# Products by channel with both parts of x in one matmul of 512 columns

## The chip, the cores and the metric

The kernel runs on one core of a Trainium2 chip. The metric is the device time of one execution in microseconds (us). The engines are named as in the profile: PE is TensorE's matmuls, PEld its weight loads, DVE is VectorE, ACT is ScalarE, POOL is GpSimd, SP the engine that issues the loads of weights.

## The reference

Two layers over 256 tokens of width 1024; each layer is a feed-forward block, a mixer and a second feed-forward block, and a norm ends it:

```python
for i in range(DEPTH):                      # DEPTH = 2
    h = h + 0.5 * swiglu_ffn(rmsnorm(h, norm_ffn1[i]), w_ffn1_in[i], w_ffn1_out[i])
    u = rmsnorm(h, norm_mix[i]) @ w_mix_in[i]          # 1024 -> 6232 columns
    z, xbc, dt_raw, q, k, v, q_idx, k_idx, w_idx = jnp.split(u, SPLIT_POINTS, axis=-1)
    y_ssd = ssd_mixer(z, xbc, dt_raw, conv_w[i], ...)  # convolution over time, masked sums, norm by group
    y_att = dsa_mixer(q, k, v, q_idx, k_idx, w_idx, positions)   # attention on the top 64 keys
    h = h + jnp.concatenate([y_ssd, y_att], axis=-1) @ w_mix_out[i]
    h = h + 0.5 * swiglu_ffn(rmsnorm(h, norm_ffn2[i]), w_ffn2_in[i], w_ffn2_out[i])
return rmsnorm(h, final_norm)
```

All is float32. The part that the change touches is the product of `rmsnorm(h)` with the columns of `z` (8 tiles of 128 channels) and of `xbc` (12 tiles) in the mixer's input projection.

## The kernel before

**Weights and products.** All weights, 214 MB, come from DRAM once, in blocks of 128 x 2048 numbers. A block lands in `raw`; ACT casts it to the matmul's reduced float32 (`whi`, L128) and DVE takes what is left over (`wlo` = raw - whi, L129). The operand x is held in the same way as a high and a low part (`tT` tiles, 32 of them of 128 x 256). Each product is made of three matmuls that add up in one PSUM bank: high with high, high with low, low with high (L186 to L188 in most places).

**By token and by channel.** Most products have the tokens on the partitions of the result: x is stationary, the weights stream past, 512 columns at a time. The columns of `z` and `xbc` are made by channel: 128 channels of the weights are stationary and the 256 tokens of x stream past (L915 to L917, 8 steps of 128 rows of the weights for each tile of channels). There are ten blocks of two such tiles in a layer, 20 tiles, 40 in the kernel. The list `MIX_ORDER` sets the order of these blocks and of the products for q, k, v and the small columns between them. In the profiled execution the first layer's stretch with products by channel lies between about 212 and 290 us.

**What becomes of a tile of channels.** `gate` (for `z`, L704) and `conv` (for `xbc`, L711) multiply the bank by `rb`, the row of the norm's factors, on DVE, into SBUF; this also empties the bank. `gate` then applies a silu on ACT. `conv` makes four steps (L718 on ACT, L720 on DVE three times) and a silu (L722 on ACT) into the tile `chan`. `by_token` transposes four such tiles on PE (L731) and scales them on DVE.

**The masked sums.** `ssd` makes, for each of two groups of eight heads, two sets of masks (four heads each): rows of cumulated sums are read back from DRAM into `s` by a DMA that POOL issues (L756), ACT makes differences and exponentials (L758 to L763), DVE multiplies (L764, L765), and PE makes the products of a set with the channels (L774, L778). `finish_y` goes on as deferred steps: `gated` scales y and multiplies by the gate, `sums` adds the squares on PE (L805) and takes the root on POOL (L809), `row` spreads the two numbers over a row by PE (L815, `rT`), and `scale` multiplies (L824 on DVE), casts (L826 on ACT) and takes the low part (L827 on DVE). The result is the first half of the operand of the out product. Attention's steps (L849 to L883) make the second half.

**What sets the order.** The code is written in program order with a planner, `flow`: after each unit of the main products it runs steps that were deferred by so many units, and one step of each generator (`ssd`, `attention`, the scores), a generator going on at its `yield`. A scheduler then puts every engine's instructions into one fixed queue; the hardware runs a queue strictly in its order. PSUM has four pools of two banks: `mm` and `ac` for main products, `sd` and `tp` for side steps.

Of the kernel before, what the change touches and what calls it, by code (L numbers as in the profile page):

```python
# [9 lines left out]
FR = mybir.dt.float32r  # L10
# [5 lines left out]
P = 128  # L16
D = 1024
L = 256
# [34 lines left out]
def hybrid_kernel(  # L53
# [12 lines left out]
    tT = ctx.enter_context(tc.tile_pool(name="tT", bufs=32))  # L66
# [26 lines left out]
    def ttile():  # L93
        return tT.tile([P, L], FR, name="tT", tag="tT")
# [88 lines left out]
    def three(ps, xhl, t, whi, wlo, first, last):  # L183

        xh, xl = (v[:, t * P:(t + 1) * P] for v in xhl)
        nc.tensor.matmul(ps, xh, whi, start=first, stop=False)  # L186
        nc.tensor.matmul(ps, xh, wlo, start=False, stop=False)  # L187
        nc.tensor.matmul(ps, xl, whi, start=False, stop=last)  # L188

# [159 lines left out]
    def setup():  # L349
# [4 lines left out]
        with tc.tile_pool(name="setup", bufs=1, reuse_waits="tile") as tmp:  # L354
# [22 lines left out]
            nc.tensor.transpose(pg[:, 0:64], rows, ident[:64, :64])  # L377
            nc.vector.tensor_copy(gains, pg[:, 0:64])
            nc.tensor.transpose(pg[:, 128:248], crows, ident[:120, :120])
# [49 lines left out]
    def split_scaled(ps, parts, t):  # L429

        parts = [([v[:, t * P:(t + 1) * P] for v in hl], g, ps[:, i * P:(i + 1) * P])
# [27 lines left out]
    class Norm:  # L459
# [14 lines left out]
        def turn(self, ps, t, c, pin=lambda ins: ins):  # L474
            if self.xT is None:
                self.xT = [(ttile(), ttile()) for _ in range(KD)]
# [94 lines left out]
    def mixer(l, norm, after):  # L571
        with ExitStack() as mctx:
# [130 lines left out]
            def gate(c, ps):  # L703
                nc.vector.tensor_mul(sz[:, c], ps, rb)  # L704
                nc.scalar.activation(sz[:, c], sz[:, c], AF.Silu)


            def conv(c, ps):
                xr = ms.tile([P, L + 3], F32, name="xr", bufs=2)
                nc.gpsimd.memset(xr[:, 0:3], 0.0)  # L710
                nc.vector.tensor_mul(xr[:, 3:], ps, rb)  # L711
# [26 lines left out]
            def ssd():  # L738
# [9 lines left out]
                for g in range(G_SSD):  # L748
                    ms4 = []
                    for h0 in (0, 4):  # L750
# [15 lines left out]
                        yield  # L766
                    half = xs[:, :, 512 * g:512 * g + 512]
# [15 lines left out]
            def finish_y(g, half, pss):  # L783
# [18 lines left out]
                def sums():  # L802
# [7 lines left out]
                    flow.defer(lambda: row(rg))  # L810
# [8 lines left out]
                def scale(rT):  # L819
                    for b in range(2):  # L820
                        for i in range(2):
                            k = 4 * g + 2 * b + i
                            hi, lo = ttile(), ttile()
# [4 lines left out]
                            yT[k] = (hi, lo)  # L828
# [4 lines left out]
            def attention():  # L833
                while bias[1] is None:
                    yield
                for hg in range(0, H_ATT, 4):
# [30 lines left out]
                    for h in range(5):  # L867
                        if h:
# [6 lines left out]
                            hi, lo = ttile(), ttile()  # L875
                            nc.scalar.copy(hi, po[:, 0:L])
                            nc.vector.tensor_sub(lo, po[:, 0:L], hi.bitcast(F32))
                            yT[8 + hg + h - 1] = (hi, lo)
# [28 lines left out]
            for what in MIX_ORDER:  # L907
                if isinstance(what, int):
                    hi, lo = stream.take()
                    for j in range(2):  # L910
                        ps = main_bank(True)[:, :L]
                        for k in range(KD):
                            o = k * 256 + j * P
                            xh, xl = norm.xT[k]
                            nc.tensor.matmul(ps, hi[:, o:o + P], xh, start=(k == 0), stop=False)  # L915
                            nc.tensor.matmul(ps, hi[:, o:o + P], xl, start=False, stop=False)  # L916
                            nc.tensor.matmul(ps, lo[:, o:o + P], xh, start=False, stop=(k == KD - 1))  # L917
# [119 lines left out]
```

## Time and profile before

| | |
|---|---|
| time of three runs, median (lowest to highest) | 1207.95 us (1207.37 to 1208.33) |
| the profiled execution: its time | 1208.47 us |
| the profiled execution: its span | 1206.8 us |
| PE busy | 1192.7 us, 99% of the span |
| PEld, DVE, ACT, POOL busy | 83%, 61%, 53%, 8% |
| TensorE's granted clock, mean | 0.999 of full speed (the 2.4 GHz level) |
| data read from HBM | 212.17 MB, 177 GB/s over the span |

The span is the time from the first to the last instruction of the profiled execution. Busy time of PE is modelled and counts a matmul until its end, while the next one starts earlier; so the cost of a matmul in a row of them is read from start to start, not from its duration. A wait is the time in which an engine had nothing to run, with the work that released it.

### The profile page before, as it was taken

What the parts mean: (1) busy time and instruction counts of PE and PEld (TensorE: products, weight loads), DVE (VectorE), ACT (ScalarE), POOL (GpSimd) and SP (SyncE); (2) the same over time, 40 slices, a digit from 0 to 9 for tenths busy, and PEclk for the clock granted to TensorE, in tenths of its full rate; (3) what the DMA queues carried; (4) which work ended last, traced back from release to release, by engine and by line L of the source; (5) the groups of instructions that cost most, each with busy time, mean ns of one, the idle gap of its engine ahead of it and who ended that gap; (6) DMA issues with size and microseconds to landing.
All of it is one profiled execution on the core that took longest, in us unless ns stands there. A gap on an engine that the chain in (4) does not pass through costs nothing.

```text
span 1206.8 us, 15519 instructions
## 1 busy us (share of the span) xinstructions
PE 1192.7 (99%) x6125; PEld 1002.6 (83%) x6125; DVE 738.4 (61%) x948; ACT 634.1 (53%) x847; POOL 101.9 (8%) x206
## 2 busy tenths in 40 slices
PE   9999999999999999999999999999999999999997
PEld 7788888998777888888888888899987788888886
DVE  5645545796797555544465554467868965554544
ACT  7544435658775544443354444366478555444432
POOL 1200000502410000000000000014133000000000
PEclk9999999999999999999999999999999999999999
DMA  9565555654534465555655645466455435556550
GB/s 291 171 205 184 186 175 165 210 175 158 192 140 145 135 210 187 164 207 188 196 161 188 201 163 198 163 205 196 145 191 192 140 122 174 191 164 204 183 200 36
DMA packets 152909, 214.26 MB, mean 178 GB/s; under 512 B 8068, under 2 KB 123012, under 8 KB 152836
## 3 DMA queue, kind: packets, MB, share of 16 engines
q1 hardware_dynamic: 151108, 207.99, 52.6%
q0 software_dynamic: 1280, 4.23, 1.0%
q8 instruction: 48, 0.79, 0.3%
q10 hardware_dynamic: 448, 1.05, 0.2%
q14 instruction: 25, 0.20, 0.1%
HBM read 212.17 MB, written 1.08 MB: 177 GB/s over the span
## 4 chain that ended last, share of the span: by engine, by line
PE 89%; ACT 5%; DMA 2%; DVE 1%; issue 1%; POOL 1%; SPq 0%; POOLq 0%; ACTq 0%
PE mm L187 14%; PE mm L188 13%; PE mm L186 13%; PE ac L188 11%; PE ac L187 11%; PE ac L186 11%; PE mm L915 2%; PE ac L915 2%; PE mm L917 2%; PE ac L916 2%; PE ac L917 2%; PE mm L916 2%; PE tp L541 2%; ACT whi L128 1%; PE sd L849 1%
## 5 line engine op out<-in xcount | busy, mean ns | idle before, releaser
L129 DVE TENSOR_TENSOR wlo<-raw,whi 128x2048 fp32r<-128x2048 f32 (+3 forms) x208 | 451.7, 2176 | 325.2 <-ACT whi L128 324.4
L128 ACT CAST whi<-raw 128x2048 fp32r<-128x2048 f32 (+3 forms) x208 | 376.8, 1818 | 285.5 <-PE ac L188 193.0
L186 PE MATMUL mm<-whi,tT 128*128 128x512 f32 (+1 forms) x640 | 255.2, 399 | 0.0
L187 PE MATMUL mm<-wlo,tT 128*128 128x512 f32 (+1 forms) x640 | 247.9, 387 | 0.9 <-DVE wlo L129 0.9
L188 PE MATMUL mm<-whi,tT 128*128 128x512 f32 (+1 forms) x640 | 248.1, 388 | 0.0
L186 PE MATMUL ac<-whi,tT 128*128 128x512 f32 (+1 forms) x448 | 176.5, 394 | 0.0
L188 PE MATMUL ac<-whi,tT 128*128 128x512 f32 (+1 forms) x448 | 173.3, 387 | 0.0
L187 PE MATMUL ac<-wlo,tT 128*128 128x512 f32 (+1 forms) x448 | 173.1, 386 | 0.0
L187 PEld LDWEIGHTS mm<-wlo,tT 128*128 128x128 f32 x640 | 120.6, 188 | 24.1 <-DVE wlo L129 1.4
L188 PEld LDWEIGHTS mm<-whi,tT 128*128 128x128 f32 x640 | 120.3, 188 | 24.4
L186 PEld LDWEIGHTS mm<-whi,tT 128*128 128x128 f32 x640 | 120.6, 188 | 23.5 <-issue 1.3
L188 PEld LDWEIGHTS ac<-whi,tT 128*128 128x128 f32 x448 | 84.3, 188 | 16.4
L187 PEld LDWEIGHTS ac<-wlo,tT 128*128 128x128 f32 x448 | 84.6, 189 | 15.4 <-DVE wlo L129 0.4
L186 PEld LDWEIGHTS ac<-whi,tT 128*128 128x128 f32 x448 | 84.3, 188 | 14.7
L186 PE MATMUL ac<-whi,hT_hi 128*128 128x512 f32 x176 | 69.3, 394 | 0.0
L186 PE MATMUL mm<-whi,hT_hi 128*128 128x512 f32 x176 | 69.0, 392 | 0.0
L188 PE MATMUL ac<-whi,hT_lo 128*128 128x512 f32 x176 | 68.6, 390 | 0.0
L188 PE MATMUL mm<-whi,hT_lo 128*128 128x512 f32 x176 | 68.6, 390 | 0.0
L187 PE MATMUL mm<-wlo,hT_hi 128*128 128x512 f32 x176 | 68.5, 389 | 0.0
L187 PE MATMUL ac<-wlo,hT_hi 128*128 128x512 f32 x176 | 68.5, 389 | 0.0
L450 POOL TENSOR_TENSOR r_x<-ms_x,mhalf 128x1 f32<-128x1 f32 x12 | 6.6, 547 | 670.7 <-DVE ms_x L448 663.2
L563 ACT ACTIVATE s1k<-mm,r_x 128x256 f32<-128x256 f32 x44 | 20.7, 471 | 69.7 <-PE mm L188 69.7
(230 smaller groups left out, 1604.6 us busy)
## 6 DMA issues: line engine op xcount, KB each, us to landing
raw<-in_w_ffn_in_dram SPq DMA_DIRECT2D x172, 512.0 KB, 4.9
raw<-in_w_ffn_out_dram SPq DMA_DIRECT2D x44, 1024.0 KB, 4.9
raw<-in_w_mix_in_dram SPq DMA_DIRECT2D x44, 1024.0 KB, 5.2
raw<-in_w_mix_out_dram SPq DMA_DIRECT2D x16, 1024.0 KB, 4.8
s<-csum POOLq DMA_DIRECT2D x8, 512.0 KB, 4.1
raw<-in_w_mix_in_dram SPq DMA_DIRECT2D x4, 600.0 KB, 3.9
raw<-in_w_mix_in_dram SPq DMA_DIRECT2D x4, 568.0 KB, 3.9
raw<-in_w_ffn_in_dram SPq DMA_DIRECT2D x8, 256.0 KB, 6.0
```

The lines of the kernel that those rows point to most:

```text
L128: pin(nc.scalar.copy(hi[:, o], raw[:, o]))
L129: pin(nc.vector.tensor_sub(lo[:, o], raw[:, o], hi[:, o].bitcast(F32)))
L186: nc.tensor.matmul(ps, xh, whi, start=first, stop=False)
L187: nc.tensor.matmul(ps, xh, wlo, start=False, stop=False)
L188: nc.tensor.matmul(ps, xl, whi, start=False, stop=last)
L450: nc.gpsimd.tensor_tensor(r, m, mhalf, ALU.pow)
L541: nc.tensor.transpose(ps[:, f * L + t * P:f * L + (t + 1) * P], hs[:, t, f * P:(f + 1) * P], ident)
L563: nc.scalar.activation(sg, ps[:, 0:256], AF.Silu, scale=norm.r[t])
L849: nc.tensor.matmul(ps[:, j * nk:(j + 1) * nk], qT[:, hg + h0 + j, t * P:(t + 1) * P], kT[:, hg + h0 + j, 0:nk], start=True, stop=True)
L915: nc.tensor.matmul(ps, hi[:, o:o + P], xh, start=(k == 0), stop=False)
L916: nc.tensor.matmul(ps, hi[:, o:o + P], xl, start=False, stop=False)
L917: nc.tensor.matmul(ps, lo[:, o:o + P], xh, start=False, stop=(k == KD - 1))
```

## The change

The tiles of x now hold both parts side by side, so that one matmul can stream 512 columns; the memory is the same.

```diff
-    tT = ctx.enter_context(tc.tile_pool(name="tT", bufs=32))
+    tT = ctx.enter_context(tc.tile_pool(name="tT", bufs=16))
...
-    def ttile():
-        return tT.tile([P, L], FR, name="tT", tag="tT")
+    def ttiles():
+
+        both = tT.tile([P, 2, L], FR, name="tT", tag="tT")
+        return both[:, 0], both[:, 1], both
...
+    def three_by_channel(ps, xhl, whi, wlo, first, last):
+
+
+        xh, both = xhl[0], xhl[2].rearrange("p a t -> p (a t)")
+        if not first:
+            nc.tensor.matmul(ps[:, :L], wlo, xh, start=False, stop=False)
+        nc.tensor.matmul(ps, whi, both, start=first, stop=last)
+        if first:
+            nc.tensor.matmul(ps[:, :L], wlo, xh, start=False, stop=False)
+
+    def join(dst, ps):
+        nc.scalar.copy(dst, ps[:, L:])
+        nc.vector.tensor_add(dst, ps[:, :L], dst)
...
                     for j in range(2):
-                        ps = main_bank(True)[:, :L]
+                        ps = main_bank(True)
                         for k in range(KD):
                             o = k * 256 + j * P
-                            xh, xl = norm.xT[k]
-                            nc.tensor.matmul(ps, hi[:, o:o + P], xh, start=(k == 0), stop=False)
-                            nc.tensor.matmul(ps, hi[:, o:o + P], xl, start=False, stop=False)
-                            nc.tensor.matmul(ps, lo[:, o:o + P], xh, start=False, stop=(k == KD - 1))
+                            three_by_channel(ps, norm.xT[k], hi[:, o:o + P], lo[:, o:o + P], k == 0, k == KD - 1)
```

So a step of a tile of channels has two matmuls instead of three: the high part of the weights with both parts of x, 512 columns into a whole bank, and the low part with the high part of x, 256 columns into the bank's first half. The halves are added on the way out: ACT copies the second half into the target, DVE adds the first half, and the multiplication by `rb` comes after that, from SBUF to SBUF.

```diff
             def gate(c, ps):
-                nc.vector.tensor_mul(sz[:, c], ps, rb)
+                join(sz[:, c], ps)
+                nc.vector.tensor_mul(sz[:, c], sz[:, c], rb)
                 nc.scalar.activation(sz[:, c], sz[:, c], AF.Silu)
...
-                nc.vector.tensor_mul(xr[:, 3:], ps, rb)
+                join(xr[:, 3:], ps)
+                nc.vector.tensor_mul(xr[:, 3:], xr[:, 3:], rb)
```

Three side steps change their place: the second transpose of the setup goes ahead of the first one's copy, a `yield` stands between the masks and the products of a group in `ssd`, and `row` is deferred by two units instead of one.

```diff
+            nc.tensor.transpose(pg[:, 128:248], crows, ident[:120, :120])
             nc.vector.tensor_copy(gains, pg[:, 0:64])
-            nc.tensor.transpose(pg[:, 128:248], crows, ident[:120, :120])
             nc.vector.tensor_copy(convs, pg[:, 128:248])
...
                         nc.vector.tensor_mul(m1, m1, bc(cb[:, g, L:384], [P, 4, P], 1))
                         yield
+                    yield
                     half = xs[:, :, 512 * g:512 * g + 512]
                     pss = [bank(ac) for _ in range(2)]
...
-                    flow.defer(lambda: row(rg))
+                    flow.defer(lambda: row(rg), 2)
```

How the queues change shows at three places of the first layer. On PE, at the first group's masked sums, where `s_` with a number is a set of masks, the kernel before has the second of the two sets (the first stands 24 matmuls of the main products earlier):

```order
L188 MATMUL mm<-whi,tT 128x512
L894 MATMUL tp<-ident,s_2901 128x128 x4
L774 MATMUL ac<-s_2887,s_1648 64x256 x2
L778 MATMUL ac<-s_2887,s_1648 64x128 x2
L774 MATMUL ac<-s_2887,s_1648 64x256 x2
L778 MATMUL ac<-s_2887,s_1648 64x128 x2
L186 MATMUL mm<-whi,tT 128x512
```

and the changed kernel (L793 and L797 are these lines there, L913 is L894, L188 to L190 are L186 to L188):

```order
L190 MATMUL mm<-whi,tT 128x512
L913 MATMUL tp<-ident,s_2765 128x128 x4
L793 MATMUL ac<-s_2677,s_1632 64x256 x2
L797 MATMUL ac<-s_2677,s_1632 64x128 x2
L793 MATMUL ac<-s_2677,s_1632 64x256 x2
L797 MATMUL ac<-s_2677,s_1632 64x128 x2
L793 MATMUL ac<-s_2751,s_1632 64x256 x2
L797 MATMUL ac<-s_2751,s_1632 64x128 x2
L793 MATMUL ac<-s_2751,s_1632 64x256 x2
L797 MATMUL ac<-s_2751,s_1632 64x128 x2
L188 MATMUL mm<-whi,tT 128x512
```

Both sets now stand together, where only the second one stood.

On ACT, after the evacuation of k's products (L944), the kernel before makes the masks of the second group (L758 to L763), squares y (L796), and evacuates a product that frees the bank for v (the L944 near the end):

```order
L758 ACTIVATE s_3047<-s_3047,cs 128x128 x2
L760 ACTIVATE s_3047<-s_3047,cs 128x256 x2
L758 ACTIVATE s_3047<-s_3047,cs 128x128 x2
L760 ACTIVATE s_3047<-s_3047,cs 128x256
L796 ACTIVATE s_1647<-s_1648 128x512
L760 ACTIVATE s_3047<-s_3047,cs 128x256
L763 ACTIVATE s_3047<-s_3047 128x512
L762 ACTIVATE s_3047<-s_3047 128x1024
L796 ACTIVATE s_1647<-s_1648 128x512
L944 ACTIVATE s_3061<-mm,r_x 128x512
L128 CAST whi<-raw 128x2048 x2
```

and the changed kernel (L960 is L944, L776 and L778 are L758 and L760, L815 is L796, L130 is L128, L914 is L895):

```order
L778 ACTIVATE s_2968<-s_2968,cs 128x256
L776 ACTIVATE s_2968<-s_2968,cs 128x128
L130 CAST whi<-raw 128x2048
L815 ACTIVATE s_1631<-s_1632 128x512
L778 ACTIVATE s_2968<-s_2968,cs 128x256
L130 CAST whi<-raw 128x2048
L914 COPY s_1633<-tp 128x4x128
L776 ACTIVATE s_2968<-s_2968,cs 128x128 x2
L778 ACTIVATE s_2968<-s_2968,cs 128x256 x2
L781 ACTIVATE s_2968<-s_2968 128x512
L780 ACTIVATE s_2968<-s_2968 128x1024
L960 ACTIVATE s_2982<-mm,r_x 128x512
```

The two casts of weights now stand among the masks, ahead of that evacuation, instead of behind it.

On ACT at the end of v's products, the kernel before has the casts of the scaled y (L826) among the evacuations of v (L941):

```order
L941 ACTIVATE s_1651<-mm,r_x 128x512
L826 CAST tT<-s_1648 128x256 x2
L128 CAST whi<-raw 128x2048
L826 CAST tT<-s_1648 128x256
L796 ACTIVATE s_1647<-s_1648 128x512
L128 CAST whi<-raw 128x2048
L826 CAST tT<-s_1648 128x256
```

and the changed kernel (L845 is L826, L957 is L941, L878 is the exponential of a softmax):

```order
L957 ACTIVATE s_1635<-mm,r_x 128x512 x2
L815 ACTIVATE s_1631<-s_1632 128x512 x2
L130 CAST whi<-raw 128x2048
L878 ACTIVATE s_3165,ssum<-s_3165,nmax 128x128 x4
L130 CAST whi<-raw 128x2048
L845 CAST tT<-s_1632 128x256
L957 ACTIVATE s_1635<-mm,r_x 128x512
L845 CAST tT<-s_1632 128x256 x3
```

The casts of y have moved behind all but the last evacuation of v, and behind two casts of weights and four exponentials.

## Rows read from the trace of the kernel before

**Rows 1.** The page: the span, and busy time of the engines.
```profile
span 1206.8 us, 15519 instructions
...
PE 1192.7 (99%) x6125; PEld 1002.6 (83%) x6125; DVE 738.4 (61%) x948; ACT 634.1 (53%) x847; POOL 101.9 (8%) x206
```

**Rows 2.** Waits of PE: who waited for whom, us in total, times, longest.
```profile
PE sd L815 <- POOL r_y L809: 1.8, 2, 0.9
PE sd L379 <- DVE gains L378: 1.1, 1, 1.1
...
PE ac L774 <- DVE s L764: 1.0, 2, 0.5
PE mm L187 <- DVE wlo L129: 0.9, 1, 0.9
PE tp L894 <- POOL s L427: 0.8, 2, 0.4
```

**Rows 3.** PE's timeline: start, duration in us, then the instruction.
```profile
227.81 0.28 PE L915 MATMUL mm<-tT,whi 128*128 128x256 f32 x1
227.93 0.28 PE L916 MATMUL mm<-tT,whi 128*128 128x256 f32 x1
...
320.10 0.39 PE L187 MATMUL mm<-wlo,tT 128*128 128x512 f32 x1
320.33 0.40 PE L188 MATMUL mm<-whi,tT 128*128 128x512 f32 x1
```

**Rows 4.** L915: count, duration in ns (min/median/max), first and last start.
```profile
L915 PE MATMUL ac<-tT,whi x160: 278/283/368, 212.1 to 876.3; 128*128 128x256 f32 x160
```

**Rows 5.** Groups on DVE and ACT, 205 to 340: count, busy us, mean ns.
```profile
L711 DVE TENSOR_TENSOR xr<-mm,rb 128x256 f32<-128x256 f32 x6 | 2.5, 418 | 0.0
...
L799 DVE TENSOR_TENSOR s<-s 128x256 f32<-128x256 f32 x1 | 0.4, 416 | 0.0
...
L903 ACT COPY rb<-sd 128x256 f32<-128x256 f32 x1 | 0.4, 372 | 0.9 <-PE sd L901 0.9
```

**Rows 6.** Busy us (instructions) of PE, PEld, DVE, ACT, POOL in two stretches.
```profile
217.00:252.00 35.00, 35.00 (x300) 34.86 (x301) 26.68 (x42) 23.09 (x32) 13.40 (x34) 1.00 0.65 205
252.00:275.00 23.00, 23.00 (x168) 21.57 (x165) 22.13 (x58) 11.60 (x17) 1.59 (x7) 1.00 0.53 161
```

**Rows 7.** PE's timeline at two of the waits, with the instruction ahead.
```profile
361.94 0.40 PE L188 MATMUL mm<-whi,tT 128*128 128x512 f32 x1
363.21 0.71 PE L815 MATMUL sd<-ident,r_y 128*128 128x128 f32 x4 [0.88 <-POOL r_y L809]
...
896.53 0.50 PE L186 MATMUL mm<-whi,tT 128*128 128x512 f32 x1
897.89 0.50 PE L187 MATMUL mm<-wlo,tT 128*128 128x512 f32 x1 [0.85 <-DVE wlo L129]
```

**Rows 8.** ACT's timeline around the start of the out product.
```profile
340.89 0.41 ACT L826 CAST tT<-s 128x256 fp32r<-128x256 f32 x1 [2.72 <-DVE s L824]
...
354.89 0.40 ACT L859 ACTIVATE s<-s,nmax 128x128 f32<-128x128 f32 x1 [0.92 <-DVE nmax L856]
...
356.77 1.91 ACT L128 CAST whi<-raw 128x2048 fp32r<-128x2048 f32 x1 [0.23 <-PE mm L188]
```

**Rows 9.** POOL's and DVE's timeline in the channel products.
```profile
210.17 0.34 POOL L425 TENSOR_TENSOR s1k<-s,ss_idx 128x72 f32<-128x72 f32 x1
...
220.42 2.40 POOL L425 TENSOR_TENSOR s1k<-s,ss_idx 128x72 f32<-128x72 f32 x1
...
220.33 2.29 DVE L129 TENSOR_TENSOR wlo<-raw,whi 128x2048 fp32r<-128x2048 f32 x1 [0.26 <-ACT whi L128]
```

**Rows 10.** The masks' DMA (count, KB, us to landing), and ACT's timeline during k and v.
```profile
s<-csum POOLq DMA_DIRECT2D x8, 512.0 KB, 4.1
...
328.11 3.71 ACT L128 CAST whi<-raw 128x2048 fp32r<-128x2048 f32 x2
...
336.43 0.68 ACT L944 ACTIVATE s<-mm,r_x 128x512 f32<-128x512 f32 x1
```

More of the change, by code (lines that the diff above doesn't have):

```diff
@@ L183, in three @@
     def three(ps, xhl, t, whi, wlo, first, last):
-        xh, xl = (v[:, t * P:(t + 1) * P] for v in xhl)
+        xh, xl = (v[:, t * P:(t + 1) * P] for v in xhl[:2])
         nc.tensor.matmul(ps, xh, whi, start=first, stop=False)
@@ L429, in split_scaled @@
     def split_scaled(ps, parts, t):
-        parts = [([v[:, t * P:(t + 1) * P] for v in hl], g, ps[:, i * P:(i + 1) * P])
+        parts = [([v[:, t * P:(t + 1) * P] for v in hl[:2]], g, ps[:, i * P:(i + 1) * P])
                  for i, (hl, g) in enumerate(parts)]
@@ L475, in turn @@
             if self.xT is None:
-                self.xT = [(ttile(), ttile()) for _ in range(KD)]
+                self.xT = [ttiles() for _ in range(KD)]
             for i in range(4):
@@ L822, in scale @@
                             k = 4 * g + 2 * b + i
-                            hi, lo = ttile(), ttile()
+                            hi, lo, both = ttiles()
                             nc.vector.scalar_tensor_tensor(y[:, b, i], y[:, b, i], gain(3, l, k), rT,
@@ L827, in scale @@
                             nc.vector.tensor_sub(lo, y[:, b, i], hi.bitcast(F32))
-                            yT[k] = (hi, lo)
+                            yT[k] = (hi, lo, both)
                 flow.defer(gated)
@@ L874, in attention @@
                                              start=False, stop=True)
-                            hi, lo = ttile(), ttile()
+                            hi, lo, both = ttiles()
                             nc.scalar.copy(hi, po[:, 0:L])
                             nc.vector.tensor_sub(lo, po[:, 0:L], hi.bitcast(F32))
-                            yT[8 + hg + h - 1] = (hi, lo)
+                            yT[8 + hg + h - 1] = (hi, lo, both)
                         if h < 4:
```

## The prediction

> **What bounds the kernel now.** I read the page first, then the waits of TensorE, then single stretches of the timeline. The page shows one bound: PE is busy 1192.7 of 1206.8 us, 99% of the span, and ACT and DVE stand at 53% and 61% [rows 1]. So only two things can move the time: what PE has to do, and the gaps in which it waits. The waits table gives the gaps by line [rows 2]; the five that matter are 1.8 us at L815, 1.1 at L379, 1.0 at L774, 0.9 at L187 and 0.8 at L894. The rest of the span is PE at work, so an instruction that is added on ACT or DVE costs nothing unless it becomes the reason for a gap. That is the whole question here: the change takes work from PE and hands more to ACT and DVE.
>
> **The matmuls.** What does one matmul cost beyond its columns? Start to start, matmuls of 256 columns follow each other by 120 ns (227.81 to 227.93), matmuls of 512 columns by 227 ns (320.10 to 320.33, by the unrounded starts 226.7) [rows 3]. The difference, 106.7 ns for 256 columns, leaves 120 - 106.7 = 13.3 ns that every matmul costs whatever its width. The columns streamed stay the same: three times 256 before, 512 and 256 after. So each step of a channel tile goes from 360 to 346.7 ns. There are 320 such steps: L915 has 160 on tiles of one pool [rows 4] and as many on the other. 320 x 13.3 ns = 4.27 us, all of it on PE, so all of it counts.
>
> The Trainium skill, "TensorE: Matmul & The Clock Gate", section "Back-to-back issue gap", speaks against so much: it gives columns by the clock plus 2.5 ns for one matmul, by which 320 fewer would be worth 0.8 us. This trace disagrees, at 13.3 ns, and I go by the trace.
>
> **The new side work.** For each of the 40 channel tiles ACT copies 256 columns out of PSUM and DVE adds the other half; the multiplication that did the evacuation stays, now from SBUF. Neighbours: such a copy on ACT took 372 ns (L903), a two-input step of 256 columns on DVE 418 ns from PSUM (L711) and 416 ns from SBUF (L799) [rows 5]. That makes 20 x 0.37 = 7.4 us on ACT and 20 x 0.42 = 8.4 us on DVE in each layer. In the first part of the channel products, 217 to 252, DVE is busy 26.7 of 35 us and ACT 23.1, so there is room. In 252 to 275 DVE is busy 22.1 of 23 us [rows 6]: what is added there is pushed back, and what is behind it in DVE's queue is the low part of the next weights. There it runs far enough ahead (the wait at L187 is a single one, in the other half of the program [rows 2]), so I cost the load itself at nothing; if that cover is gone, each us of DVE beyond it is a us of PE.
>
> **The waits that go.** At two places I read the gap from start to start: L815 begins 1.27 us after the matmul before it, L187 1.36 us [rows 7]; less 0.23 for the matmul that is 1.05 and 1.13, where the idle alone is 0.88 and 0.85 [rows 2, 7]. So a gap costs about 1.2 times what the table shows. I expect four of the five lines to go.
> - L379: the second transpose of the setup no longer stands behind the DVE copy that reads the same bank.
> - L815: the row comes a unit later, so GpSimd's power (L809) has time.
> - L774: the first set of four heads' products now runs directly ahead of the second, and fills the wait for the second's mask.
> - L187 (second layer): the exponentials now sit together on ACT, which saves a pair of table loads ahead of the casts, and the low part comes earlier.
>
> Together 1.1 + 1.8 + 1.0 + 0.9 = 4.8, by 1.2 = 5.8 us over both layers (bounds 3 and 6). L894 I leave as it is.
>
> **The waits that come.** The steps that are moved later have to be finished later, and four places get a wait in each layer.
> - The start of the out product. Its first operand is the row's scaled y, which was ready some 20 us ahead and is now made on the spot. Call T the end of the last v product. ACT's queue holds there a cast (1.91, the buffer is free at T - 3), the four exponentials of a softmax (from 354.89 to the cast at 356.77 less 0.23 of idle, 1.65), a second cast whose buffer comes free at T, and then the copy (0.41) that PE waits for [rows 8]. T - 3 + 1.8 + 1.7 is T + 0.5; the cast ends at T + 2.3, the copy at T + 2.7. PE has about 1.5 us of small products to fill that: 1.2 us of wait. The low part of that operand stands on DVE behind the second low part of the weights (2.29 [rows 9]), to T + 5.1, where eight matmuls carry PE to T + 4.5: 0.6 more. Sum 1.8, bounds 0 and 2.6 (that cast and the low part not covered at all).
> - The second v product. The masks of the second group are read from DRAM once the first set's products are done, now some 6 us later, and that takes 4.1 us to land. Behind them on ACT are two casts, the masks and the evacuation that frees the bank; in the kernel before that stretch takes 8.3 us (328.11 to 336.43) [rows 10]. I get 1.0 us, bounds 0 and 2.0.
> - The second group's row, in the out product: transposes, scaling and copy in one chain, 0.3, bounds 0 and 1.05 (what L815 costs now).
> - The second half of q's product, the transposes of the first channels, and the rotation: each waits for an ACT step that stands behind new copies; 0.4 together, bounds 0 and one cast, 1.9.
>
> That is 3.5 us in a layer, 7.0 in both (bounds 0 and 15.1). **The sum:** 4.27 + 5.8 - 7.0 = 3.1 us. The profiled execution took 1208.47 us, of which 1206.8 is its span [rows 1] and 1.7 lies around it, and would go to 1205.4; the median is 0.5 lower, 1207.95, so I put the forecast at 1204.9.
>
> **Rivals.**
> 1. *The cover holds.* If ACT gets through its queue ahead of PE at all four places, both savings stay: 10.1 us, 1197.9. For it: ACT is idle almost half the time. Against: the wait at the start of the out product comes from an order, a cast that cannot begin before T, and not from load.
> 2. *Slower: ACT's queue is one cast late.* The added copies come in the queue ahead of casts, and each operation that PE waits for is behind a cast. If the queue arrives one cast later than I reckon (1.9 us [rows 8]) at the second v product and at the start of the out product, in both layers, that is 4 x 1.9 = 7.6 us more: 1212.5. It makes the kernel slower than the bound once each of the four is over 1.4 us late. For it: DVE has no room in 252 to 275 [rows 6], and ACT's steps of the convolution wait for DVE. Against: PE's own new waits give the queue time to catch up.
> 3. *The saving on the matmuls isn't there*, because the 13.3 ns are not the matmul's but the step's. Then 4.27 goes, or all but 0.8: 1208.4 to 1209.2. Against it: 256 and 512 columns differ by just what the columns explain.
> 4. *GpSimd is held up.* The same GpSimd operation on 72 columns took 0.34 us at 210.17 and 2.40 at 220.42, where it ended with a low part of the weights that DVE had started at 220.33 and that reads two tensors in SBUF [rows 9]. The multiplications by channel now read two tensors in SBUF too. If the four rotation operations of a tile each lose one of them, 4 x 0.42 = 1.7 us, and PE waits for it once in each layer, the gain shrinks by 3.4: 1208.3. For it: PE already waits for the rotation at L894 [rows 2].
>
> The Trainium skill, "SBUF — State Buffer", section "Who interferes with whom", says that a VectorE instruction with two SBUF inputs and a GpSimd instruction that reads SBUF exclude each other. The trace agrees, with the 2.40 against 0.34.
>
> **Chances.** A measurement of this kernel can tell about 0.2% (2.4 us) from no change. The forecast 0.52 (its own range 1201.5 to 1208: 0.33 faster, 0.17 the same, 0.02 slower), rival 1 0.14 (faster), rival 2 0.17 (0.15 slower, 0.02 the same), rival 3 0.05 (the same), rival 4 0.12 (0.10 the same, 0.02 slower). Faster 0.47, the same 0.34, slower 0.19. The range reaches into rivals 1 and 2 until about a tenth is left out at each end: 1199.5 to 1210.
>
> **What would show it.** In the profile after: the 512-column matmul and the 256-column one of a channel step 347 ns together; no wait of PE at the setup's transposes, none at the row on GpSimd, none at the second set of heads; new waits on ACT's copy of y at the first matmul of the out product and, for its low part, on DVE; one of PE on ACT's evacuation at the second v product. The prediction is wrong if the out product starts without a wait, if the low part of the weights is late in the channel products, or if new waits pass 12.5 us in all.

## The result: 1220 us, 12.4 us slower

| | before | after |
|---|---|---|
| median (lowest to highest) | 1207.66 us (1207.18 to 1208.33) | 1220.05 us (1218.62 to 1222.31) |
| ratio, 95% interval | 1 | 1.0104 (1.0086 to 1.0121) |
| the profiled execution: time, span | 1208.47, 1206.8 us | 1220.37, 1218.7 us |
| TensorE's granted clock, mean | 0.999 | 0.995 |

The forecast was 1204.9 with a range to 1210. The time lies outside, on the slow side.

The page after, its span and the busy times, against [rows 1]:

```profile
span 1218.7 us, 14983 instructions
...
PE 1192.8 (98%) x5805; PEld 986.6 (81%) x5805; DVE 752.9 (62%) x988; ACT 640.9 (53%) x883; POOL 95.2 (8%) x206
```

The 320 matmuls are gone (6125 to 5805). DVE is 14.5 us busier, ACT 6.8: 40 copies more, and four table loads of 1.28 us less, the pairs that the prediction saw saved. PE is as busy as before, although it has less to do. The waits of PE after, against [rows 2]: who waited for whom, us in total, times, longest.

```profile
PE sd L834 <- DVE tT L896: 6.3, 2, 3.2
PE tp L673 <- POOL s L443: 4.0, 2, 2.0
PE tp L900 <- DVE s L882: 2.6, 2, 1.3
PE ac L793 <- DVE s L782: 1.4, 2, 0.7
...
PE tp L676 <- POOL s L668: 1.0, 2, 0.5
...
PE mm L190 <- DVE tT L846: 0.6, 2, 0.3
```

L834, the second group's row, was L815; L673 and L676 are the transposes of the index columns; L900 and L190 stand at the start of the out product; L793 was L774. L379 and the second layer's L187 [rows 2] are gone from the list, and L815's wait for GpSimd's power with them.

**Where the time went.** I added up every gap of PE of more than 0.35 us, from start to start as in [rows 7]. They come to 7.9 us before and 20.8 us after, 12.9 more; the saved matmuls give 3.2 back (below), and a slower clock behind the longest waits takes 3.6 (below). That is 13.3 more. The last matmul of the profiled execution starts 11.9 us later (1199.63 to 1211.52), so these entries carry the loss and 1.4 us more, which smaller gaps, not followed here, give back:

| place, both layers | before | after |
|---|---|---|
| setup, L379 | 1.3 | 0 |
| index transposes, L673 and L676 | 0 | 5.7 |
| second set of heads, L774 / L793 | 1.3 | 1.8 |
| out product, L900 and L190 | 0 | 3.9 |
| second group's row, L815 / L834 | 2.1 | 6.6 |
| L187 of the second layer | 1.1 | 0 |

**The row.** PE's timeline, then ACT's and DVE's (start, duration in us, instruction):

```profile
376.67 0.38 PE L892 MATMUL sd<-s,s 128*128 128x128 f32 x2
380.21 1.20 PE L834 MATMUL sd<-ident,r_y 128*128 128x128 f32 x4 [3.15 <-DVE tT L896]
```

```profile
375.50 1.90 ACT L130 CAST whi<-raw 128x2048 fp32r<-128x2048 f32 x1
377.30 0.65 ACT L895 CAST tT<-sd 128x256 fp32r<-128x256 f32 x2
...
377.43 2.29 DVE L131 TENSOR_TENSOR wlo<-raw,whi 128x2048 fp32r<-128x2048 f32 x1 [1.68 <-ACT whi L130]
379.64 0.75 DVE L896 TENSOR_TENSOR tT<-sd,tT 128x256 fp32r<-128x256 f32 x2
```

The row's four matmuls need a bank of the pool `sd`. In PE's queue they now stand right behind the two pairs of heads of attention (L890, L892), whose results fill both banks. A bank is free when ACT has cast it (L895) and DVE has taken the low part (L896). ACT does that behind a cast of weights, DVE behind the low part of the same weights. GpSimd's root, for which L815 waited, had been done since 368.2. PE waits 3.15 us, in the middle of the stretch where nothing else of its queue may go ahead.

**The clock behind it.** Stretches of 2 us, two in the first layer and one in the second: busy us of PE, PEld, DVE, ACT and POOL, then PEclk, the granted clock.

```profile
380.00:382.00 2.00, 1.79 (x8) 1.82 (x9) 0.95 (x4) 0.04 (x1) 0.00 (x0) 0.55 0.55 113
382.00:384.00 2.00, 2.00 (x10) 1.82 (x9) 2.00 (x6) 1.15 (x3) 0.00 (x0) 0.60 0.99 408
...
984.00:986.00 2.00, 2.00 (x8) 1.71 (x7) 2.00 (x6) 1.01 (x3) 0.00 (x0) 0.50 0.80 330
```

The granted clock stands at half, the 1.2 GHz level, for 3.4 us in the first layer, from the end of the wait (380.18), and for 6.8 us in the second, from 0.9 us ahead of its end (980.93). There PE's matmuls of 512 columns start 0.43 us apart (984.95 to 985.37 us) where 0.227 is usual. The loss can be read against e14 (below), whose PE has the same instructions in this stretch and the same wait at the row, but no half clock behind it in the profiled execution (its row, and the 2 us from 378 on):

```profile
378.26 0.68 PE L837 MATMUL sd<-ident,r_y 128*128 128x128 f32 x4 [3.15 <-DVE tT L899]
...
378.00:380.00 2.00, 1.62 (x13) 1.47 (x13) 1.47 (x5) 0.51 (x2) 0.00 (x0) 1.00 0.46 86
```

From the row's first matmul to the 60th after it PE takes 13.28 and 14.44 us in the changed kernel (first and second layer), and 12.05 and 12.06 us in e14. So the half clock cost 1.2 and 2.4 us.

**The index columns.** PE, then POOL, which makes their rotation (L440 to L443, L668):

```profile
227.09 0.66 PE L673 MATMUL tp<-ident,s 128*128 128x128 f32 x4 [2.02 <-POOL s L443]
228.24 0.33 PE L676 MATMUL tp<-ident,s 128*128 128x128 f32 x1 [0.50 <-POOL s L668]
```

```profile
222.74 0.10 POOL L727 MEMSET xr<- 128x3 f32 x1 [21.36 <-DVE s1k L738]
222.79 0.50 POOL L440 TENSOR_TENSOR s1k<-s,cc_idx 128x144 f32<-128x144 f32 x1
...
224.49 2.54 POOL L443 TENSOR_TENSOR s<-s1k 128x144 f32<-128x144 f32 x1
...
224.07 2.61 DVE L131 TENSOR_TENSOR wlo<-raw,whi 128x2048 fp32r<-128x2048 f32 x1 [0.50 <-ACT whi L130]
```

Before, the rotation began at 209.59. Now GpSimd stands idle for 21.36 us, at the memset that clears the edge of a convolution's tile, and does the whole rotation after it, late. At its late place its last step for the first tile (L443), for which PE waits, runs beside a low part of weights on DVE and takes 2.54 us, where the same step took 0.49 us before (at 217.38). With 0.49 it would have ended near 225.0, about when PE came to the transposes; that is an estimate, and no run takes this overlap away at the late place. Its queue shows why (as built, before and after; L424 and L440 are the first operation of a tile's rotation):

```
before                                 after
L710 MEMSET xr x2                      L727 MEMSET xr x2
L450 TENSOR_TENSOR r_x x2              L466 TENSOR_TENSOR r_x x2
L424 TENSOR_TENSOR s1k<-s,cc_idx       L727 MEMSET xr
L425 TENSOR_TENSOR s1k<-s,ss_idx       L440 TENSOR_TENSOR s1k<-s,cc_idx
L426 TENSOR_TENSOR s1k<-s,ss_idx       L441 TENSOR_TENSOR s1k<-s,ss_idx
L424 TENSOR_TENSOR s1k<-s,cc_idx       L442 TENSOR_TENSOR s1k<-s,ss_idx
L427 TENSOR_TENSOR s<-s1k              L440 TENSOR_TENSOR s1k<-s,cc_idx
L710 MEMSET xr                         L443 TENSOR_TENSOR s<-s1k
```

The third memset, which waits for the first convolution to be done with its tile, has moved ahead of the rotation.

**The matmuls.** PE's timeline in a channel tile, against [rows 3]:

```profile
213.83 0.28 PE L197 MATMUL mm<-tT,wlo 128*128 128x256 f32 x1
213.94 0.40 PE L198 MATMUL mm<-tT,whi 128*128 128x512 f32 x1
214.18 0.28 PE L197 MATMUL mm<-tT,wlo 128*128 128x256 f32 x1
```

Start to start 117 ns from a 256 to the next 512 and 233 ns back: 350 ns for a step, where the sum said 346.7 and three matmuls took 360. So a matmul less saves 10 ns, not 13.3, and 320 of them 3.2 us, not 4.27.

### The profile page after: what moved, and what is told of

It is laid out like the page before. It is cut to its first block, busy times and chain, and to the rows that moved or that the text cites. A ratio compares the mean times of both kernels' runs of the same rounds, so it can differ in the third digit from the quotient of the medians.

```text
span 1218.7 us, 14983 instructions
## 1 busy us (share of the span) xinstructions
PE 1192.8 (98%) x5805; PEld 986.6 (81%) x5805; DVE 752.9 (62%) x988; ACT 640.9 (53%) x883; POOL 95.2 (8%) x206
## 3 DMA queue, kind: packets, MB, share of 16 engines
q10 hardware_dynamic: 448, 1.05, 0.2%
## 4 chain that ended last, share of the span: by engine, by line
PE 89%; ACT 3%; DVE 3%; POOL 2%; issue 1%; DMA 1%; POOLq 0%; SPq 0%; ACTq 0%
PE mm L188 14%; PE mm L190 14%; PE mm L189 14%; PE ac L190 11%; PE ac L189 11%; PE ac L188 11%; PE mm L198 2%; PE ac L198 2%; ACT whi L130 2%; PE tp L557 2%; DVE wlo L131 2%; PE mm L197 1%; PE ac L197 1%; PE sd L868 1%; PE tp L495 1%
## 5 line engine op out<-in xcount | busy, mean ns | idle before, releaser
L130 ACT CAST whi<-raw 128x2048 fp32r<-128x2048 f32 (+3 forms) x208 | 376.9, 1818 | 288.8 <-PE ac L190 179.5
L188 PE MATMUL mm<-whi,tT 128*128 128x512 f32 (+1 forms) x640 | 256.0, 400 | 0.4 <-ACT s L960 0.3
L190 PE MATMUL mm<-whi,tT 128*128 128x512 f32 (+1 forms) x640 | 247.4, 388 | 0.6 <-DVE tT L846 0.6
L188 PE MATMUL ac<-whi,tT 128*128 128x512 f32 (+1 forms) x448 | 176.8, 395 | 0.0
L190 PE MATMUL ac<-whi,tT 128*128 128x512 f32 (+1 forms) x448 | 172.3, 385 | 0.0
L188 PEld LDWEIGHTS mm<-whi,tT 128*128 128x128 f32 x640 | 120.9, 189 | 25.2 <-issue 1.7
L190 PEld LDWEIGHTS mm<-whi,tT 128*128 128x128 f32 x640 | 120.4, 188 | 25.9 <-DVE tT L846 1.4
L190 PEld LDWEIGHTS ac<-whi,tT 128*128 128x128 f32 x448 | 84.2, 188 | 16.6
L188 PEld LDWEIGHTS ac<-whi,tT 128*128 128x128 f32 x448 | 84.2, 188 | 14.8 <-ACT tT L450 0.2
L188 PE MATMUL ac<-whi,hT_hi 128*128 128x512 f32 x176 | 69.3, 394 | 0.0
L188 PE MATMUL mm<-whi,hT_hi 128*128 128x512 f32 x176 | 69.1, 392 | 0.0
L190 PE MATMUL ac<-whi,hT_lo 128*128 128x512 f32 x176 | 68.6, 390 | 0.0
L190 PE MATMUL mm<-whi,hT_lo 128*128 128x512 f32 x176 | 68.6, 390 | 0.0
L198 PE MATMUL mm<-tT,whi 128*128 128x512 f32 x160 | 57.5, 400 | 0.0
```

The lines of the kernel that those rows point to most:

```text
L130: pin(nc.scalar.copy(hi[:, o], raw[:, o]))
L198: nc.tensor.matmul(ps, whi, both, start=first, stop=last)
```

## The experiments

Twelve kernels, each timed against the kernel before on the same chip. The first four take the change apart: three kernels with parts of it undone, and one with the side steps alone.

**e1_row1**: the changed kernel, the row deferred by one unit again.

```diff
-                    flow.defer(lambda: row(rg), 2)
+                    flow.defer(lambda: row(rg))
```

> The changed kernel with the row deferred by one unit again, the extra yield kept. Theory of place (the loss comes from where the row of the scaled y now stands, and from GpSimd's queue): the first group's row is back ahead of the out product, so the waits at its start (1.5 + 0.5 us per layer) go, and the second group's row asks for its bank ahead of attention's second pair, so most of the 3.3 us wait and the half clock after it go (6.6 + 4.4 us in all); about 2 us come back at the row's new place. 1220 - 3.9 - 6.6 - 4.4 + 2 = 1207. Theory of load (40 copies and 40 additions make ACT and DVE late wherever the steps stand): the waits move elsewhere, 1216 to 1220.

Measured: 1215.92 us, ratio 1.0065 (1.0050 to 1.0080). That is 4 us better than the changed kernel, not the 13 expected. Its waits of PE, and the timeline of PE and DVE at the row:

```profile
PE tp L673 <- POOL s L443: 4.0, 2, 2.0
PE mm L188 <- ACT tT L845: 3.9, 2, 1.9
PE sd L834 <- DVE tT L896: 1.8, 2, 0.9
```

```profile
374.92 0.68 PE L834 MATMUL sd<-ident,r_y 128*128 128x128 f32 x4 [0.89 <-DVE tT L896]
...
375.02 2.28 DVE L131 TENSOR_TENSOR wlo<-raw,whi 128x2048 fp32r<-128x2048 f32 x1
377.22 1.26 DVE L843 SCALAR_TENSOR_TENSOR s<-s,gains,sd 128x256 f32<-128x256 f32 x3
...
378.18 0.80 PE L188 MATMUL mm<-whi,tT 128*128 128x512 f32 x1 [1.93 <-ACT tT L845]
```

A unit earlier the row still waits for its bank, though less, and the low part of the weights (2.28 us) now gets ahead of the scaling of y, so that the matmul which takes the scaled y waits as well. Its profile also has the half clock, for 6.8 us from 377.41, in the second of these waits. So the deferral alone isn't the cause.

**e2_noyield**: the changed kernel without the `yield`, the row still deferred by two.

```diff
-                    yield
                     half = xs[:, :, 512 * g:512 * g + 512]
```

> The changed kernel without the extra yield between masks and products, the row still deferred by two units. Theory of place: the unit that the yield costs is what carries the first group's row to the start of the out product, so those waits go (3.9 us); the second group's row stands one attention pair earlier and waits about 1 us instead of 3.3, without losing the clock: 1220 - 3.9 - 4.6 - 4.4 = 1207. If the deferral by two alone is the fault, the row still waits over 2 us: 1213 or more. Theory of load: 1216 to 1220.

Measured: 1210.67 us, ratio 1.0022 (1.0012 to 1.0031). Both the row's wait and those at the start of the out product are gone, 9.4 us. The `yield` moves the whole of `finish_y` back; a row that is deferred by two units costs nothing as long as that isn't added to it. Left is the wait for the rotation, which this expectation left out:

```profile
PE tp L673 <- POOL s L443: 4.0, 2, 2.0
...
PE tp L676 <- POOL s L668: 1.0, 2, 0.5
```

**e3_mm**: the matmuls, the joins and the setup's transposes alone, both side steps in `ssd` undone (the diffs of e1 and e2 together).

> The changed kernel with both side steps undone: only the matmuls with 512 columns, the joins and the setup's transposes are left of the change. Theory of place: before, less 3.2 us for the matmuls (350 instead of 360 ns a step in the trace after) and 0.8 for the setup, plus 5.7 for the wait for the rotated index columns (2.15 + 0.68 us per layer, GpSimd's memset standing ahead of the rotation), which stays: 1207.7 - 4.0 + 5.7 = 1209.4. Theory of load: most of the loss stays, 1216 to 1219.

Measured: 1210.90 us, ratio 1.0031 (1.0021 to 1.0041). The part meant to save PE's time is by itself slower than before. PE waits 4.0 us at L673 and 1.0 at L676, as in e2, and for GpSimd's root as before (1.8 us).

**e4_moves**: the kernel before with the three moved side steps, no change of a matmul.

```diff
+            nc.tensor.transpose(pg[:, 128:248], crows, ident[:120, :120])
             nc.vector.tensor_copy(gains, pg[:, 0:64])
-            nc.tensor.transpose(pg[:, 128:248], crows, ident[:120, :120])
...
+                    yield
                     half = xs[:, :, 512 * g:512 * g + 512]
...
-                    flow.defer(lambda: row(rg))
+                    flow.defer(lambda: row(rg), 2)
```

> The kernel before with the three moved side steps alone; three matmuls by channel and no joins. Theory of place: the waits of the row and at the start of the out product appear here too, without the new load: 1207.7 - 0.8 + 3.9 + 6.6 + 4.4 - 2.1 (the old wait of the row) - 1.3 (the old wait of the second set) = 1218. Theory of load: 1205 to 1208, since no work was added.

Measured: 1215.74 us, ratio 1.0066 (1.0051 to 1.0081). At the row, the out product and the second set of heads PE waits as in the changed kernel, to the tenth, and there is no wait for the rotation:

```profile
PE sd L816 <- DVE tT L878: 6.3, 2, 3.2
PE tp L882 <- DVE s L864: 2.6, 2, 1.3
PE ac L775 <- DVE s L764: 1.4, 2, 0.7
...
PE mm L188 <- DVE tT L828: 0.6, 2, 0.3
```

The wait at L187 of the second layer is still there (0.90 us). With e3 this splits the loss in two parts that nearly add up: 3.2 us in e3 and 8.1 here, 11.3 of 12.4. The moved steps bring the waits at the row and the out product, with the old matmuls as with the new: the added load on ACT and DVE is no part of it. The joined matmuls bring the wait for the rotation, with the side steps moved or not.

**The rotation: first theory.** GpSimd's queue suggested that the memset holds the rotation up. The next four kernels have no memset among the convolutions: two fixed tiles whose edges are cleared once, in the setup. e5 is that in the changed kernel, e6 in e2, e7 in e3, and e8, the control, in the kernel before.

```diff
+    xrs = [const.tile([P, L + 3], F32, name=f"xr{i}") for i in range(2)]
+    xr_turns = iter(range(1000))
...
+    for xr in xrs:
+        nc.gpsimd.memset(xr[:, 0:3], 0.0)
...
-                xr = ms.tile([P, L + 3], F32, name="xr", bufs=2)
-                nc.gpsimd.memset(xr[:, 0:3], 0.0)
+                xr = xrs[next(xr_turns) % 2]
```

> The changed kernel with two fixed tiles for the convolution's input, whose three zero columns are set once at the start, so that GpSimd's queue has no memset for each tile of channels. Theory of queue (in the changed kernel the memset for the third tile waits for DVE's convolution steps on the first and stands ahead of the rotation of the index columns): the rotation starts some 8 us earlier, PE's waits for it (2.15 + 0.68 us per layer) go, 1220.0 - 5.7 = 1214.3. Rival, contention (the rotation is slow because DVE's operations with two inputs in SBUF hold it up): the waits stay, 1219 to 1220.

> The run without the extra yield (1210.7) and without the memsets. Theory of queue: the waits for the rotation go (5.7 us), and with them the half clock that followed them in some executions (up to 2 us): from 1209.2 to 1209.4, the executions at the higher mean clock, to 1203.5, which is 0.35% faster than before. Rival, contention: 1210.

> Only the matmuls with 512 columns, the joins and the setup's transposes, without the memsets. Theory of queue: from 1210.1 to 1210.4 (the executions at a mean clock of 0.999) to 1204.5: before, less 3.2 us for the matmuls and up to 0.8 for the setup, with both waits of the row on GpSimd left. If joins and additions cost more than the waits that the trace names: 1206 or more. Rival, contention: 1210.

> The kernel before without the memsets: the control. Its rotation does not stand behind a memset that waits, so nothing is gained: 1207.2 to 1208.2. If the memsets cost by themselves, as much as in the changed kernel: 1203 to 1205.

Measured: e5 1219.64 (1.0095, 1.0079 to 1.0111), e6 1209.20 (1.0005, 0.9996 to 1.0014), e7 1210.93 (1.0024, 1.0014 to 1.0034), e8 1207.86 (1.0000, 0.9991 to 1.0009). Each of the first three was expected 5.3 to 6.4 us faster than it came out. The theory fell: without any memset the wait is still there, and the times lie within 1 us of those of the rival, contention. One row of e6, GpSimd in the rotation, names another releaser (ACT's L743 is the silu that ends a convolution):

```profile
224.79 2.13 POOL L445 TENSOR_TENSOR s1k<-s,ss_idx 128x72 f32<-128x72 f32 x1 [8.44 <-ACT bcs L743]
```

The rotation's two temporary tiles come from the ring `s1k`, five tiles that it shares with the accumulators of the convolutions. A tile of the ring is handed out again when the accumulator in it has been read, that is at the end of a convolution.

**Second theory: the shared ring.** e10 is e2 with the rotation of the index columns on two halves of a 512-column tile of another ring (`two()`, which the index scores and attention use, among others).

```diff
-    def rope(eng, v, t, which, nh):
+    def rope(eng, v, t, which, nh, m=None):
...
-        m1 = row1k()
-        m2 = row1k()
+        if m is not None:
+            m1, m2 = m[:, 0:256], m[:, 256:512]
+        else:
+            m1 = row1k()
+            m2 = row1k()
...
-                    rope(nc.gpsimd, idx_tm[:, t, 0:576].rearrange("p (h c) -> p h c", h=9), t, "idx", 9)
+                    rope(nc.gpsimd, idx_tm[:, t, 0:576].rearrange("p (h c) -> p h c", h=9), t, "idx", 9, two())
```

> The run without the extra yield (1210.7), with one edit: the rotation of the index columns takes its two temporary tiles from the ring of the 512-column tiles, not from the ring of five that the convolutions' sums use too; the memsets stay. Theory of the shared ring (in the runs without memsets GpSimd idled 8.44 us before the rotation of the second token tile, released by ACT's silu of the first tile of channels, which gives a temporary tile back and now comes a cast later): the rotation runs at 208 to 220 as in the kernel before, PE's waits at the index transposes (2.2 + 0.7 us per layer) go and so does the half clock after them: from 1209.3, the executions at the higher mean clock, to 1203.6. Rival, contention (DVE's operations with two inputs in SBUF hold GpSimd up): at least 1.5 us per layer of the wait stay, 1206 to 1210.

Measured: **1202.27 us**, ratio 0.9954 (0.9941 to 0.9966), 8.4 us faster than e2 and outside the 1206 to 1210 of contention alone. POOL's last step of the second tile's rotation, then PE's transposes, and what is left of the waits:

```profile
217.41 0.24 POOL L671 COPY s<-s 128x64 f32<-128x64 f32 x1
...
225.23 0.60 PE L676 MATMUL tp<-ident,s 128*128 128x128 f32 x4
```

```profile
PE tp L915 <- POOL s L446: 1.1, 4, 0.4
...
PE ac L795 <- DVE s L785: 1.0, 2, 0.5
```

The rotation is done 7.6 us ahead of PE. The memsets are still in this kernel; in its queue the third one stands behind the rotation again.

**e13_gate_first**: e2, the ring shared as before, but in the order of the products a tile pair of `z` (negative numbers) goes ahead of the first pair of `xbc`, so that the first convolution asks for its accumulator later.

```diff
-    MIX_ORDER = ["idx0", "idx1", 8, -8, -6, 10, 0, -4, -2, 2, 4, "q0", 6, "q1", "k0", "k1", "v0", "v1"]
+    MIX_ORDER = ["idx0", "idx1", -8, 8, -6, 10, 0, -4, -2, 2, 4, "q0", 6, "q1", "k0", "k1", "v0", "v1"]
```

> The run without the extra yield, with the first two blocks of channels exchanged: a block of z goes first, whose tiles need no temporary tile of the ring, and the first block of the convolution second. Theory of the shared ring: the rotation gets its temporary tiles before the convolutions take theirs, the waits at the index transposes go too, 1203 to 1205.5 (the convolution's channels come 5.6 us later for the masked sums, which costs nothing there). Rival, contention: 1209 to 1211.

Measured: **1201.99 us**, ratio 0.9952 (0.9940 to 0.9964). GpSimd ends the second tile's rotation at the same place as in e10:

```profile
217.21 0.24 POOL L668 COPY s<-s 128x64 f32<-128x64 f32 x1
```

So the wait needs both: the shared ring, and convolutions that take their tiles of it before the rotation does. Either remedy takes it away, though a step of the rotation still runs beside DVE's low part in both kernels (2.61 us at 213.50 in e10, 2.62 at 213.29 in e13): the overlap costs PE only where the rotation is late.

**e14_after_ring** and **e15_mm_ring**: the ring of e10 in the changed kernel, and in e3.

> The changed kernel with the index rotation's temporary tiles from the other ring, yield and deferral as changed. Shared ring: the 5.7 us of the index transposes go, the waits of the row with the half clock after them stay: 1220.0 - 5.7 = 1214.3. Contention: 1218 to 1220.

> Only the matmuls with 512 columns, the joins and the setup's transposes, with the rotation's temporary tiles from the other ring. Shared ring: from 1210.2 (the executions at a mean clock of 0.999) less 5.7: 1204.5, 3.2 us under before, which is what the matmuls save; both waits of the row on GpSimd (2.1 us) are left, which sets it 1 to 2 us above the run without the yield. Contention: 1208 to 1210.

Measured: e14 1212.85 (1.0040, 1.0027 to 1.0054), e15 1204.54 (0.9972, 0.9962 to 0.9983). e14 keeps the waits of e4 (6.3 and 2.6 us), e15 the one for GpSimd's root (1.8). The half clock that e14 was expected to keep is missing in two of its four executions (mean clock 0.998: 1211.2 and 1211.8 us; at 0.996: 1213.9 and 1214.2), so the two lines with e14 below hold to about 1.5 us. With them the change can be taken apart in medians:

| step | from | us |
|---|---|---|
| matmuls, joins, setup's transposes, without the ring's wait | e15 against before | -3.2 |
| the row deferred by two units, alone | e10 against e15 | -2.3 |
| the `yield`, with the row deferred by two | e14 against e10 | +10.6 |
| the ring's wait | after against e14 | +7.2 |
| sum | | +12.3 |

The change measured +12.4. The parts depend on the order in which they are taken: with the row deferred by one unit the `yield` costs 5.0 us (e1 against e3), not 10.6. The ring's wait alone is 6.4 (e3 against e15) to 8.4 us (e2 against e10). The best kernels, e10 and e13, are 0.46% and 0.48% faster than before: all of the change but the `yield`, and the rotation freed.

**Why the order turned.** This part is read from the traces; no run separates it. ACT's timeline at the first convolution, before and after:

```profile
217.70 0.60 ACT L718 ACTIVATE s1k<-xr,convs 128x256 f32<-128x256 f32 x1 [1.74 <-DVE xr L711]
218.39 1.91 ACT L128 CAST whi<-raw 128x2048 fp32r<-128x2048 f32 x1
...
220.71 0.40 ACT L722 ACTIVATE bcs<-s1k 128x256 f32<-128x256 f32 x1
```

```profile
216.50 1.91 ACT L130 CAST whi<-raw 128x2048 fp32r<-128x2048 f32 x1 [2.45 <-PE mm L198]
218.31 0.60 ACT L736 ACTIVATE s1k<-xr,convs 128x256 f32<-128x256 f32 x1
...
222.13 1.91 ACT L130 CAST whi<-raw 128x2048 fp32r<-128x2048 f32 x1 [2.49 <-PE ac L198]
223.95 0.41 ACT L740 ACTIVATE bcs<-s1k 128x256 f32<-128x256 f32 x1
```

Before, the first step (L718, now L736) ran ahead of the cast and the silu (L722, now L740) ahead of the next one; now each stands behind a cast. The join puts a copy, an addition and a multiplication where one multiplication was, and the convolution's steps miss their places by a cast, the silu by 3.2 us on the span's clock, although the changed kernel is 1.9 us ahead when the tile leaves its bank (L711 at 217.25 before, L204 at 215.38 after). A ring's tile that waits for that silu comes as much later. e3 has the wait and e4 has not, so it comes with the new matmuls and joins; whether the copy, the addition or PE's faster steps tip it was not tried.

## Why the prediction was wrong, step by step

**The second group's row: 0.3 a layer, bounds 0 to 1.05. Wrong, the largest error.** It measured 3.3, and 1.2 and 2.4 us of slower clock behind it were not in the sum. I costed the row as a chain of its own steps, transposes to scaling to copy, and took the upper bound from what L815 waited for before. But a moved instruction waits for whatever is ahead of it at its new place, its PSUM bank too. Two units later, behind attention's pairs, both banks of `sd` were taken, and their release hung on a cast of weights on ACT and a low part on DVE, 1.9 and 2.3 us that stood in the trace of before [rows 8, 9].

**The rotation: part of a term of 0.4 a layer. Wrong.** It measured 2.85 (2.19 and 0.66). I listed the wait for ACT behind new copies, bounded by one cast, but never followed the rotation's temporary tiles to those that share their ring, nor read GpSimd's queue, where the memset's move stood before any run. Rival 4 named the place, the effect (PE waits for GpSimd's rotation) and half of the mechanism: L443 took 2.54 us at 224.49 beside a low part on DVE, as in [rows 9], and about 2 of PE's 2.85 us are that overlap, by the estimate above. What it lacked is the late start. In e10 an operation of the rotation takes 2.61 us as well, at 213.50, and no one waits. It also looked to the multiplications by channel, where it is the low part of the weights that runs beside L443.

**The start of the out product: 1.8 a layer. Right** in place and size, and half in its path: 1.48 at L900 and 0.45 at L190, 1.9 together, where 1.2 and 0.6 were forecast:

```profile
359.24 0.41 PE L900 MATMUL tp<-ident,s 128*128 128x128 f32 x2 [1.31 <-DVE s L882]
...
362.08 0.73 PE L190 MATMUL mm<-whi,tT 128*128 128x512 f32 x2 [0.29 <-DVE tT L846]
...
359.22 0.40 ACT L845 CAST tT<-s 128x256 fp32r<-128x256 f32 x1
```

The low part on DVE (L190) is as forecast. The first wait falls not on the matmul that takes y, but on attention's transposes just ahead of it (L900), which wait for DVE's scaling of the softmax (L882), behind a low part of weights; that path was not in the prediction. The forecast path, ACT's copy of y behind the second cast, ends at 359.62, and the matmul that takes it starts at 359.68, so PE would have stood until then by it alone. That two paths end within 0.6 us of each other is luck.

**The second v product: 1.0 a layer. Too much.** One gap of 0.45 us, in the second layer (L188, waiting for ACT's L960). The queue had more room than I gave it.

**The waits that go: 5.8. Three of the four lines went,** L379, L815's wait for GpSimd and L187. The wait at L187 went by the mechanism named, as far as the traces show: the kernels with the new matmuls have four table loads less (14, not 18) and no wait for a low part over 0.5 us, while e4, with the moved steps alone, keeps all 18 and the wait. So it is the matmuls and joins that bring it, not the moved steps. The wait at L774 stayed and grew, from 0.66 to about 0.9 a layer: both sets stand together, but the first of them does not fill the time until the second's mask. L815 shows the limit of such a list: the wait for GpSimd did go, and a longer one took its place at the same instruction.

**The matmuls: 4.27. The mechanism was right, the size is 3.2.** 13.3 ns came from rows of equal matmuls [rows 3]; 256 and 512 columns in turn lose 10.3 and 19.7 ns (117 and 233 ns where, by the same difference of rows, 106.7 and 213.3 are columns), 30 together where the sum had two times 13.3. The Trainium skill, "TensorE: Matmul & The Clock Gate", section "Back-to-back issue gap", has 2.5 ns beyond the columns for an isolated matmul, by which the estimate was 0.8 us in all; the 10 ns measured here stand nearer to the first reading of the trace. Rival 3 did not come true.

**The new side work: nothing. Right as a load, wrong as a delay.** Copies on ACT took 362 ns and the steps on DVE 418 and 431, about as costed (two groups after, 205 to 340 us: count, busy us, mean ns):

```profile
L204 DVE TENSOR_TENSOR xr<-mm,xr 128x256 f32<-128x256 f32 x6 | 2.5, 418 | 0.0
...
L203 ACT COPY xr<-mm 128x256 f32<-128x256 f32 x6 | 2.2, 362 | 1.3 <-PE mm L198 1.3
```

No low part of weights came late in the channel products. What they cost is the order: three steps in a chain where one stood, and with it a place in ACT's queue. Nor is the cost quite nothing without the ring's wait: e15 saves 3.2 us, where the matmuls (3.2) and the waits at L379 (1.3) and L187 (1.1) make 5.6. The other 2.4 us are not found in one place. In the profiles the last matmul of e15 starts 3.9 us earlier than before (1195.78): 3.2 from the matmuls and 1.9 from gaps over 0.35 us (two new ones of 0.58 and 0.39 us take part of the 2.4 back), less 1.3 in smaller gaps, which I have not followed one by one.

**Rival 2** had the right sign, at 0.17, and a mechanism, a step that comes one cast late, that is found at another place: it looked for it at the second v product and the out product; it happened at the first convolution. At the row's bank, too, PE waits behind a cast, but there the moved row brings it and not the added copies: e4 has no copies and the same wait. The prediction's own test, that it is wrong "if new waits pass 12.5 us in all", is what came about: 5.7 at the index columns, 3.9 at the out product and 6.6 at the row make 16.2.

## What to carry to other kernels

A step that is moved waits at its new place for everything that its queue and its buffers hold there: go through the PSUM bank and the ring of each tile that it takes, name who releases it, and look for casts on the way. A tile ring that two chains share ties them together, so that a step added to one can stall the other on an engine that nobody touched; read the queues of all engines after a change, the idle ones first, for an instruction that has passed another. When a change comes as a bundle, split it before judging it: here the parts are worth, in the order of the table, -3.2, -2.3 and +10.6 us, and a stall of 7.2 that giving one tile another ring takes away.

## What had not been expected of the hardware

**The clock falls behind a wait, in some executions.** In the kernel before PE has no wait as long as these, and no stretch at half clock until its last matmul is done. After the waits at the row (3.15 us in the profile) the granted clock of the changed kernel stood at half for 3.4 and 6.8 us; the profiled execution of e14 has the same waits and no half clock. The shorter waits for the rotation (2.02 and 0.50 us, close together) are followed by it in some executions only, too: the profiled execution of e2 has 3.4 us of it behind them in each layer (at 227.94 and 825.27), that of e3 none. The four executions of e3 at a mean granted clock of 0.999 took 1210.1 to 1210.4 us; those at 0.996 took 1212.9 to 1213.5. The kernels with either wait vary by 1.3 to 3.7 us, those with neither (before, e8, e10, e13, e15) by 0.4 to 1.8. A wait of PE can so cost more than its length, by 1.2 to 2.4 us here. Why the same wait is followed by it in one execution and not in another stays open.

**A 512-column matmul next to one of 256 columns** costs a little more than two of a kind: 350 ns for the pair, where 120 and 227 would be 347.
